# Two more 2 MB stretches of a rotation kernel's stores written with 8 KB rows in place of 16 KB

## The chip, the cores and the metric

The kernel runs on one core of one Trainium2 chip. The metric is the device time of one execution in microseconds (us), and the time of a kernel is the median of its runs. One execution was also recorded by the hardware profiler; its page and trace are what this text reads.

## The reference

```python
def setup_inputs():
    batch, c, h, w = 32, 3, 256, 256
    return {"x": np.random.randn(batch, c, h, w).astype(np.float32)}

def reference(x):
    return np.rot90(x, k=-1, axes=(-2, -1)).astype(np.float32)
```

Each of the 96 images of 256 x 256 float32 is turned by a quarter: 25.17 MB are read, the same number of bytes is written, and nothing is calculated.

## The kernel before

**Tiling.** The rows of all images are one list, `(b c h) w`. With R = 16 rows of an image to a partition, a *slab* is 128 partitions x 4096 elements (E), 16 KB on each partition and 2 MB in all. The 12 slabs stand in five groups of 2, 2, 2, 4 and 2 slabs (`sizes`), and each group has an SBUF tile of its own (`groups[n]`, `u` in the profile) that is loaded, turned in place and stored. So all 25 MB fit, and no buffer is used twice.

**Loads** are all issued by SyncE (SP) at the start. Group 0 comes in three DMAs with 8 KB rows (L55, L56: two of 1 MB, one of 2 MB). The others come with one DMA of 2 MB for each part of the partitions (L66), with rows of 16 KB, or 32 KB in the four-slab group; the very last is split in two of 1 MB (L63, L64). A row here is one contiguous run of bytes, and the trace shows one DMA packet for each.

**Turning.** VectorE transposes 32 x 32 blocks (L72, L88, L93). The first quarter of a slab pair goes to a spare tile, as its place is still needed, and ScalarE copies it back at the end (L78, L98). A group can be stored when VectorE and ScalarE are through with it. The four-slab group has eight such copies, the others fewer.

**Stores** are issued by SP in the order of the groups, each group in two halves: `a` is the parity of the partition (`groups[n][a::2]`, 64 partitions). For a two-slab group a half is 2 MB, for the four-slab group 4 MB, and its rows are 16 KB, the whole of a slab on one partition (L117). Only the first half of group 0 is split, in two stores of 1 MB that each write 8 KB rows, first the lower half of every slab's columns and then the upper (L109). The first store of all also waits for the last load but one (`mark`), so that stores do not push in among loads.

**What orders the DMAs.** All 25 DMAs go out on SP's one queue, in program order. The framework gives them eight semaphores in turn, so from the ninth on each DMA waits for the one eight places before it. SP ends (L143) with a row of wait instructions on these semaphores, and then a gather and release among the engines ends the program.

Of the kernel before, what the change touches and what calls it, by code (L numbers as in the profile page):

```python
# [1 line left out]

# [4 lines left out]


@with_exitstack  # L10
def kernel(
    ctx: ExitStack,
    tc: tile.TileContext,
    x: bass.AP,
    out: bass.AP,
):

    nc = tc.nc
    fp32 = mybir.dt.float32

    B, C, H, W = x.shape
    P = nc.NUM_PARTITIONS
    R = 16  # L30
    E = R * W
    hw = R // 2
    low, high = slice(0, hw), slice(hw, R)

    rows_in = x.rearrange("b c h w -> (b c h) w")
    rows_out = out.rearrange("b c h w -> (b c h) w")

    sizes = (2, 2, 2, 4, 2)
    first = [sum(sizes[:n]) for n in range(len(sizes))]
    groups = [  # L40
        ctx.enter_context(tc.tile_pool(name=f"group{n}", bufs=1)).tile([P, s, E], fp32, name=f"u{n}")
        for n, s in enumerate(sizes)
    ]
    psum = ctx.enter_context(tc.tile_pool(name="psum", bufs=1, space=bass.MemoryType.PSUM))
    spare = [psum.tile([P, E // 2], fp32, name=f"spare{h}") for h in range(2)]
    extra = ctx.enter_context(tc.tile_pool(name="extra", bufs=1)).tile([P, E // 2], fp32, name="extra")

    def rows_of(rows, n):
        return rows[first[n] * P * R : (first[n] + sizes[n]) * P * R]


    ld = rows_of(rows_in, 0).rearrange("(s i p r) w -> s i p (r w)", s=2, i=2, p=P)
    home = [groups[0][:, s].rearrange("p (i f) -> p i f", i=2) for s in range(2)]
    for i in range(2):
        nc.sync.dma_start(out=home[0][:, i], in_=ld[1, i])  # L55
    nc.sync.dma_start(out=home[1], in_=ld[0].transpose([1, 0, 2]))  # L56
    for n in range(1, len(sizes)):
        I = sizes[n]
        ld = rows_of(rows_in, n).rearrange("(a i m r) w -> i m a (r w)", a=2, i=I, m=P // I)
        to = groups[n].rearrange("p s f -> p (s f)").rearrange("p (a f) -> p a f", a=2)  # L60
        for i in range(I):
            if (n, i) == (len(sizes) - 1, I - 1):
                mark = nc.sync.dma_start(out=to[i::I, 0], in_=ld[i][:, 0])  # L63
                nc.sync.dma_start(out=to[i::I, 1], in_=ld[i][:, 1])  # L64
            else:
                nc.sync.dma_start(out=to[i::I], in_=ld[i])  # L66

    def turn_slab(src, dsts):
        s = src.rearrange("p (i r g c) -> p c r g i", i=2, r=R // 2, c=R)
        for h, d in enumerate(dsts):  # L70
            d = d.rearrange("p (c k r) -> p c r k", c=hw, r=R // 2)[:, :, ::-1, ::-1]
            nc.vector.transpose(out=d, in_=s[:, h * hw : (h + 1) * hw])  # L72

    u = groups[0]
    turn_slab(u[:, 0], spare)
    turn_slab(u[:, 1], [u[:, 0, : E // 2], u[:, 0, E // 2 :]])
    for h in range(2):
        nc.scalar.copy(out=u[:, 1, h * E // 2 : (h + 1) * E // 2], in_=spare[h])  # L78

    def turn_group(n, held):  # L80
        I = sizes[n]
        T = I // 2
        K = W // (R * T)
        u = groups[n].rearrange("p s f -> p (s f)")
        src = u.rearrange("p (a t r g c) -> p t c r g a", a=2, t=T, r=R, c=R)
        dst = u.rearrange("p (i c k t r) -> p t c r k i", i=I, c=R, k=K, t=T)[:, ::-1, :, ::-1, ::-1, :]
        for t in range(T):
            nc.vector.transpose(  # L88
                out=held[t].rearrange("p (i c k r) -> p c r k i", i=I, c=hw, k=K)[:, :, ::-1, ::-1, :],
                in_=src[:, t, low, low])  # L90
        for c, r in ((low, high), (high, high), (high, low)):
            for t in range(T):
                nc.vector.transpose(out=dst[:, t, c, r], in_=src[:, t, c, r])  # L93
        back = u.rearrange("p (i c k t r) -> p t i c k r", i=I, c=R, k=K, t=T)[:, ::-1]
        for t in range(T):
            kept = held[t].rearrange("p (i c k r) -> p i c k r", i=I, c=hw, k=K)
            for i in range(I):
                nc.scalar.copy(out=back[:, t, i, low, :, high], in_=kept[:, i])  # L98

    for n, held in enumerate(([extra], [spare[1]], spare, [extra]), 1):  # L100
        turn_group(n, held)


    st = rows_of(rows_out, 0).rearrange("(s i m r) w -> i m s (r w)", s=2, i=2, m=P // 2)
    for a in range(2):

        for f in ((low, high) if a == 0 else (slice(0, R),)):
            f = slice(f.start * W, f.stop * W)
            put = nc.sync.dma_start(out=st[a][:, :, f], in_=groups[0][a::2, :, f])  # L109
            if f.start or a:  # L110
                continue
            tc.add_manual_dep(put.ins, mark.ins.name, mybir.DependencyInfo(
                mybir.DependencyClass.Sync, mybir.DependencyReason.SCHED_ONLY), reason="stores after loads")
    for n in range(1, len(sizes)):
        st = rows_of(rows_out, n).rearrange("(a i m r) w -> a m i (r w)", a=2, i=sizes[n], m=P // 2)
        for a in range(2):
            nc.sync.dma_start(out=st[a], in_=groups[n][a::2])  # L117


# [1 line left out]
_INS = ['x']  # L121
_OUTS = [((32, 3, 256, 256), 'float32')]


# [23 lines left out]
```

## Time and profile before

| | |
|---|---|
| median of 3 runs | 123.1 us (123.0 to 123.1) |
| the profiled execution | 123.22 us |
| its span | 121.4 us |
| VectorE busy | 87.4 us, 24 instructions |
| ScalarE busy | 14.9 us, 17 instructions |
| DMA packets | 3600, of them 400 under 512 B |
| bytes moved | 50.33 MB, mean 414 GB/s over the span |
| time of the packets | 97.7% of 16 DMA engines' span |
| first store issued | 59.47 us |
| last store issued | 98.71 us |

The busy table gives each engine's time and share of the span. The slices cut the span in 40 and give each engine's busy share in tenths; the DMA row is the mean over the core's 16 DMA engines. The waits say who waited for whom, with the total, the number and the longest; "SPq" is SP's sequencer, which issues the DMAs. The view of DMA issues gives size and the time from issue to landing, which includes the time in which a DMA stands behind others in the queue.

### The profile page before, as it was taken

To read this page: it belongs to the slowest core of one execution; us is meant where nothing else is said; L and a number is where in the kernel's file an instruction comes from. 1 tells how busy PE (TensorE), PEld (TensorE's weight loads), DVE (VectorE), ACT (ScalarE), POOL (GpSimd) and SP (SyncE) were. 2 spreads that over 40 slices of the span, in tenths; PEclk is the share of its full clock that TensorE was granted. 3 is DMA by queue.
4 is the path that set the end of the run, shared out by engine and by line. 5 is a ranking of instruction groups with operands and counts; after the bars stand their busy time and mean duration, and the time that the engine had idled before them with its cause. 6 is when DMAs were issued, how large, how long until landed. Compare 5 with 4: busy or idle time off the path is not lost.

```text
span 121.4 us, 132 instructions
## 1 busy us (share of the span) xinstructions
DVE 87.4 (72%) x24; ACT 14.9 (12%) x17; POOL 0.2 (0%) x4
## 2 busy tenths in 40 slices
DVE  0039999999999999999999999999999600000000
ACT  0000400380005100060000000327000320000000
POOL 0000000000000000000000000000000000000000
DMA  3999999999989898999989999999999999999994
GB/s 70 432 429 426 456 432 432 432 432 432 518 345 518 345 518 345 432 432 432 426 378 453 432 432 432 432 432 432 405 416 426 432 432 432 432 432 432 432 426 178
DMA packets 3600, 50.33 MB, mean 414 GB/s; under 512 B 400, under 2 KB 400, under 8 KB 400
## 3 DMA queue, kind: packets, MB, share of 16 engines
q1 hardware_dynamic: 3600, 50.33, 97.7%
HBM read 25.17 MB, written 25.17 MB: 414 GB/s over the span
## 4 chain that ended last, share of the span: by engine, by line
DVE 66%; issue 6%; DMA 6%; ACT 1%; ACTq 1%; SPq 0%; DVEq 0%
DVE u L93 39%; DVE spare L88 9%; DVE extra L88 6%; DVE u L72 6%; DVE spare L72 6%; DMA u<-in_x_dram 6%; ACT u L98 1%; ACTq L143 1%; SPq L55 0%; DVEq L88 0%; DVEq L72 0%
## 5 line engine op out<-in xcount | busy, mean ns | idle before, releaser
L93 DVE STREAM_TRANSPOSE u<-u 128x2048 f32<-128x2048 f32 x15 | 54.4, 3651 | 0.4
L72 DVE STREAM_TRANSPOSE spare<-u 128x2048 f32<-128x2048 f32 x2 | 7.1, 3585 | 8.2 <-DMA u<-in_x_dram 8.2
L98 ACT COPY u<-spare 128x512 f32<-128x512 f32 (+1 forms) x10 | 6.0, 688 | 38.5 <-DVE u L93 38.5
L88 DVE STREAM_TRANSPOSE spare<-u 128x2048 f32<-128x2048 f32 x3 | 10.7, 3585 | 0.0
L88 DVE STREAM_TRANSPOSE extra<-u 128x2048 f32<-128x2048 f32 x2 | 8.0, 4011 | 0.0
L72 DVE STREAM_TRANSPOSE u<-u 128x2048 f32<-128x2048 f32 x2 | 7.8, 3986 | 0.0
L98 ACT COPY u<-extra 128x1024 f32<-128x1024 f32 x4 | 4.0, 1043 | 22.8 <-DVE u L93 22.8
L78 ACT COPY u<-spare 128x2048 f32<-128x2048 f32 x2 | 3.6, 1871 | 8.7 <-DVE u L72 8.7
L78 ACT ACT_TABLE_LOAD x1 | 1.3, 1283 | 13.1 <-DMA u<-in_x_dram 13.1
L132 POOL MEMSET const-bfloat16-1.0<- 128x1 bf16 x1 | 0.1, 101 | 0.0
L132 POOL MEMSET const-uint8-127<- 128x1 uint8 x1 | 0.1, 101 | 0.0
L132 POOL MEMSET const-float32-0.0<- 128x1 f32 x1 | 0.1, 98 | 0.2 <-issue 0.2
L132 POOL MEMSET const-float32-1.0<- 128x1 f32 x1 | 0.1, 98 | 0.0
## 6 DMA issues: line engine op xcount, KB each, us to landing
u<-in_x_dram SPq DMA_DIRECT2D x10, 2048.0 KB, 30.4
out_dram<-u SPq DMA_DIRECT2D x7, 2048.0 KB, 17.6
out_dram<-u SPq DMA_DIRECT2D x2, 4096.0 KB, 21.2
u<-in_x_dram SPq DMA_DIRECT2D x4, 1024.0 KB, 20.5
out_dram<-u SPq DMA_DIRECT2D x2, 1024.0 KB, 5.7
```

What stands on the lines that cost most here:

```text
L72: nc.vector.transpose(out=d, in_=s[:, h * hw : (h + 1) * hw])
L78: nc.scalar.copy(out=u[:, 1, h * E // 2 : (h + 1) * E // 2], in_=spare[h])
L88: nc.vector.transpose(out=held[t].rearrange("p (i c k r) -> p c r k i", i=I, c=hw, k=K)[:, :, ::-1, ::-1, :], in_=src[:, t, low, low])
L93: nc.vector.transpose(out=dst[:, t, c, r], in_=src[:, t, c, r])
L98: nc.scalar.copy(out=back[:, t, i, low, :, high], in_=kept[:, i])
L132: nc = _bacc.Bacc("TRN2", target_bir_lowering=False, num_devices=1)
L143: with _tile.TileContext(nc) as tc:
```

## The change

The stores of groups 1 to 4 are issued by this loop. For the four-slab group (n = 3) and the last group (n = 4), the first two slabs of the first half are now stored as two DMAs of 1 MB, each with half of every slab's columns, so with 8 KB rows. What is left of the half, two slabs of the four-slab group and nothing of the last group, goes out as one store with 16 KB rows. The second halves, and groups 0, 1 and 2, are as before. There are 28 DMAs in place of 25.

```diff
     for n in range(1, len(sizes)):
-        st = rows_of(rows_out, n).rearrange("(a i m r) w -> a m i (r w)", a=2, i=sizes[n], m=P // 2)
+        I = sizes[n]
+        st = rows_of(rows_out, n).rearrange("(a i m r) w -> a m i (r w)", a=2, i=I, m=P // 2)
         for a in range(2):
-            nc.sync.dma_start(out=st[a], in_=groups[n][a::2])
+            done = 0
+            if a == 0 and n >= 3:
+
+                done = 2
+                for f in (slice(0, E // 2), slice(E // 2, E)):
+                    nc.sync.dma_start(out=st[a][:, :done, f], in_=groups[n][a::2, :done, f])
+            if done < I:
+                nc.sync.dma_start(out=st[a][:, done:], in_=groups[n][a::2, done:])
```

## The prediction

> **What bounds the kernel now.** I read the page's busy table and its slices first: they say which engine is short of time. VectorE is busy 72% and is done by slice 32; the DMA row has a 9 or an 8 in every slice but the first and last.
>
> ```profile
> DVE 87.4 (72%) x24; ACT 14.9 (12%) x17; POOL 0.2 (0%) x4
> ...
> DVE  0039999999999999999999999999999600000000
> ...
> DMA  3999999999989898999989999999999999999994
> ...
> q1 hardware_dynamic: 3600, 50.33, 97.7%
> ```
>
> The packets of the one queue take 97.7% of 16 DMA engines' span. So the kernel is bound by moving 50.33 MB, and the page's chain (which follows VectorE and stops at 98 us) is not the chain that sets the end. What waits at the end is in the waits of SP's queue:
>
> ```profile
> SPq L109 <- DMA u<-in_x_dram: 31.2, 1, 31.2
> SPq L117 <- DVE u L93: 22.8, 2, 13.3
> SPq L143 <- DMA out_dram<-u: 20.3, 2, 19.6
> ```
>
> SP's last act (L143) is to wait 19.6 us at a stretch for stores that are long issued. Its timeline says when the last four stores, the ones that the change touches, were issued:
>
> ```profile
> 84.37 15.74 SPq L117 DMA_DIRECT2D out_dram<-u  x4
> ```
>
> And the view of DMA issues, asked for one issue at a time, says how long each took to land. The four rows are the store issued at 66.64 (the last one ahead of the four-slab group), the four-slab group's first half (issued 84.37), its second half (85.02) and the kernel's last store (98.71):
>
> ```profile
> out_dram<-u SPq DMA_DIRECT2D x1, 2048.0 KB, 24.5
> ...
> out_dram<-u SPq DMA_DIRECT2D x1, 4096.0 KB, 16.6
> ...
> out_dram<-u SPq DMA_DIRECT2D x1, 4096.0 KB, 25.8
> ...
> out_dram<-u SPq DMA_DIRECT2D x2, 2048.0 KB, 19.8
> ```
>
> (In the last row x2 is a wait for the median of the last two: 17.6 and 21.9.) Issue plus time to landing: the store ahead lands at 66.64 + 24.5 = 91.1, so at 84.37, when the four-slab group becomes ready, the queue still holds 6.8 us of work; that group lands at 101.0 and 110.8, so at 98.06, when the last group is ready, it holds 12.7 us. The last store lands at 98.71 + 21.9 = 120.6, and the span ends at 121.4. From first load to last landing the engines are never without work: joining the trace's packet records (start, duration, size) end to end gives engines whose packets overlap by 4 to 8 ns, with no gap over 60 ns once all are running. Two things can therefore change the time: what a packet costs, and the 0.8 us behind the last landing.
>
> **The change, part by part.**
>
> *What it does to the queue.* Of the four-slab group's first 4 MB store, the first two slabs (2 MB) go as two 1 MB stores of 8 KB rows and the other 2 MB as one store of 16 KB rows; of the last group, the first 2 MB store goes as two of 1 MB, 8 KB rows. Bytes are the same. Packets follow rows: 128 rows of 16 KB become 256 of 8 KB, twice, so +256, and each of the three added DMAs adds 16 completion packets (the page has 400 under 512 B for 25 DMAs), +48: 3904 for 3600. Nothing moves on VectorE or ScalarE. In the built program, the first store of each of the two groups waits for the same VectorE and ScalarE counts as before.
>
> *Price of a row.* From the packet records, mean duration by stage: 8 KB loads (3 to 12.9 us) 309.2 ns; 8 KB stores (61.6 to 66 us) 309.4; 16 KB stores right behind those (66.8 to 84) 611.5; 16 KB at 87 to 98 us, 615.4; at 101 to 120 us, 615.7. Per engine the change turns 2 x 8 rows of 16 KB into 32 of 8 KB: 16 x (2 x 309.4 - 615.5) = 16 x 3.3 = +0.05 us. Completion packets are 9 ns each, three more per engine, at most +0.03. Landings say less: the pair of 8 KB stores of 1 MB, its extra completion packet included, landed 4.90 us after the load ahead of it (median engine), and late 2 MB stores of 16 KB land 4.90 apart, so 0. I take **+0.02**, between the two, nearer to the landings, since they hold all of it. Ends: 0 and +0.16: the dearest row of 8 KB that the trace has is the 2 MB load of L56, 4.97 us against 4.89 for the 16 KB loads, 0.08 for each of the two.
>
> *What 16 KB rows cost behind 8 KB rows.* The one thing that speaks for the change. Rows of 16 KB took 611 both times that they ran right behind 8 KB rows (loads from 13 us: 611 to 613; stores from 66.8: 611.5), and about 615.5 everywhere else. The stores stayed at 611 until about 84.4, just when SP issued the next stores, and the loads crept up from 13 to 18 us, when SP issued loads; between 87 and 120 nothing brought 611 back. I read this as: 8 KB rows put the engines in step, a burst of issues puts them out. That is a reading, not a shown cause. By it the new kernel gains 4 ns a row from the end of the 8 KB part in the four-slab group (91.1 + 4.9 = 96.0) to the next issues at 98.06, 2 us or 3.4 rows, -0.01; and for the last 2 MB, 8 rows, behind which nothing is issued, -0.03. Sum **-0.04**. Ends: 0, if it isn't so; and if issues don't undo it, 6 MB + 2 MB = 32 rows by up to 7 ns (the packets' distances fall from 614 at most to 607), -0.22.
>
> *Issues.* Three more of them on SP, 0.65 us each (L109's 8 KB stores took 672 and 650 ns); behind them waits only SP, and the queue holds 6.8 and 12.7 us of work meanwhile. Nothing, as long as that cover holds. Rows during a burst of two issues (98.0 to 100.7) took 619.7, 4 ns over the rest for 4 rows: three more issues could add 0.03; I count 0 and keep 0.03 for the upper end. From the ninth on each DMA also waits for the one eight before it; for the stores of these two groups those landed at 62 to 86 us, so before the groups are ready.
>
> The Trainium skill ("SBUF — State Buffer", section "The DMA setup-cost knee") speaks against the change: every transfer pays a roughly fixed 2 us, so one big transfer beats several. By that, three more transfers would cost an estimated 6 us, and the time would be 129. This trace differs where the queue is full: the two 1 MB loads of the last group landed 2.47 and 2.45 us after the DMA before each, half of the 4.89 of a 2 MB load. The measurement decides, and the sum has nothing for it.
>
> *Behind the last landing.* At the end SP runs five wait instructions on the eight DMA semaphores, one after the other, in a fixed order that begins with the fourth semaphore. DMAs take the eight in turn. Before, the 25th and last DMA is on the first semaphore, which stands in the fourth of the five waits; one more wait follows. With 28 DMAs the last is on the fourth semaphore, in the **first** of the five, and four waits follow the last landing: three more. Each is short but serial. In SP's instruction records the wait behind the last landing starts 35 ns after the one before ended and takes 28, 63 together; two of these waits that had nothing to wait for started 59 ns apart. 3 x 60 = **+0.18 us**, straight onto the end: SP's drain, GpSimd's gather and the release all stand behind it. Ends: 0 (if SP looks through satisfied waits while another is pending, for which no row speaks) and +0.19.
>
> *Sum.* +0.02 - 0.04 + 0.18 = **+0.16 us**. The profiled execution took 123.22 us (span 121.4 and 1.8 around it), so 123.38 by its own time; it ran 0.1 above the median of 123.1, so 123.26 by that, and I say **123.25**. That is +0.12%: less than the 0.2% (0.25 us) that a measurement of this kernel can tell from no change.
>
> **Rivals.**
> 1. *The 8 KB rows do what they seem to have done at 66 us, and it lasts.* For it: 611.5 for 17 us of stores. Against it: it ended at the next burst of issues. 32 rows at -4 to -7 ns, -0.14 to -0.22, rows +0.02, tail +0.18: -0.02 to +0.06, time 123.1.
> 2. *Same, and the tail is free.* Then -0.12 to -0.20: 122.95. Faster by over 0.2% (below 122.85) it is only with the rows at nothing and the gain at its end.
> 3. *Slower: 8 KB rows cost here what they cost in loads.* Place: the two 2 MB parts at 91 to 96 and 110.8 to 115.7 us. Price: 0.08 us each, as L56's load, +0.16 in place of +0.02; nothing regained, issues +0.03, tail +0.18: +0.37, 123.45. It decides once the two parts together cost over 0.07 us (tail 0.18, and nothing gained). Against it: the 8 KB stores at 62 to 66 us landed at the pace of 16 KB ones.
> 4. *It doesn't do what it says:* the smaller stores might have been able to leave earlier than the big one, as they need fewer copies. The built program waits for the same counts, and the queue is 6.8 us deep anyway. Time then by tail alone: 123.3 at most.
>
> **How the numbers follow.** Forecast (123.15 to 123.35, with rival 4) 0.55; rivals 1 and 2 as far as they stay between 122.85 and 123.15, 0.20; rival 2 below that, 0.03; rival 3 and all else from 123.35 up, 0.22. Faster by over 0.2%: 0.03. Slower by over 0.2%: 0.22. Within: 0.75. The range leaves out rival 2's lower part and what lies beyond rival 3: 122.95 to 123.45.
>
> **What would show it.** Right: 3904 packets, 448 of them under 512 B; SP's last wait for stores ends, and four short waits instead of one follow; landing to end of span 1.0 us for 0.8. 16 KB rows of the last 2 MB at 611. Wrong: DMA engines with gaps, so a cover that failed; 8 KB rows over 312 ns; 16 KB rows that stay at 611 past 98 us; a last landing before 120.4 or after 120.8.

## The result, and the profile after

The changed kernel takes **123.44 us** (123.36 to 123.68, 6 runs), the kernel before, beside it, 123.07 (122.95 to 123.12): a ratio of 1.0035, interval 1.0023 to 1.0048. It is slower by 0.37 us, or 0.3%: over twice the +0.16 of the forecast, which had given 0.75 to a time within 0.2% of the kernel before. The profiled execution took 123.68 us, the longest of the six, span 121.9.

The busy table and the packet counts of the page of after:

```profile
DVE 87.4 (72%) x24; ACT 14.9 (12%) x17; POOL 0.2 (0%) x4
...
DMA  3999999999989999999999999999999999999993
...
DMA packets 3905, 50.33 MB, mean 413 GB/s; under 512 B 449, under 2 KB 449, under 8 KB 449
...
q1 hardware_dynamic: 3904, 50.33, 97.6%
q14 instruction: 1, 0.00, 0.0%
```

The compute engines are as they were, and the queue is as full: 3904 packets, 448 small ones (the 3905th is an instruction fetch). So the added issues left no hole in the queue. Where the time came from is in two other views. First the DMA issues of after, one at a time: the two 8 KB stores of the four-slab group (issued at 84.33 and 84.98) and the 16 KB store behind them (86.42):

```profile
out_dram<-u SPq DMA_DIRECT2D x1, 1024.0 KB, 9.4
...
out_dram<-u SPq DMA_DIRECT2D x1, 1024.0 KB, 11.2
...
out_dram<-u SPq DMA_DIRECT2D x1, 2048.0 KB, 14.7
```

They land at 93.7, 96.2 and 101.1: 2.5 us for each 1 MB in 8 KB rows, 4.9 for the 2 MB in 16 KB rows, and the first pair of 8 KB stores, at 62 to 66 us, had taken 4.90 together. In the landing records (median engine) the two new pairs took 5.00 and 4.99, and what stands behind them 4.89 (2 MB), 9.80 (4 MB) and 4.87. In the kernel before 2 MB took 4.89 (half of the first 4 MB) and 4.90, and the second 4 MB 9.78. So the 8 KB rows cost 0.1 us a pair and gave nothing back. From the landing of the last load to that of the last store (the stores' part below) the median engine took 58.59 us before and 58.76 after, **+0.17**. (From the first load's landing to the last one's it is 56.25 to 56.26 in both.)

Second, SP's wait instructions at the program's end, first of before, then of after (number, shortest/median/longest in ns, first and last start):

```profile
L143 SPq EVENT_SEMAPHORE  x7: 17/28/9787, 100.2 to 121.4; - x7
```

```profile
L151 SPq EVENT_SEMAPHORE  x7: 17/28/28, 120.8 to 121.8; - x7
```

Before, SP went through its waits from 100.2 us on and sat 9.8 us in the fourth. After, the first wait is the long one. The view of SP's waits has it, with the total, the number and the longest:

```profile
SPq L151 <- DMA out_dram<-u: 19.4, 1, 19.4
```

So all five are passed behind the last landing at 120.82. Their starts are 58, 67, 65 and 61 ns apart. From the last landing to the end of the span it is 0.85 us before and 1.07 after, **+0.21**. Together +0.38, against the 0.37 of the medians. The two profiled spans are 0.45 apart: in that one execution the loads also landed 0.06 earlier, and the last engine came 0.13 further behind the median one. So such parts, each from one execution, are good to 0.1 or 0.2 us.

### The profile page after: what moved, and what is told of

It reads as the page before. It is cut to its first block, busy times and chain, and to the rows that moved or that the text cites. A ratio compares the mean times of both kernels' runs of the same rounds, so it can differ in the third digit from the quotient of the medians.

```text
span 121.9 us, 135 instructions
## 1 busy us (share of the span) xinstructions
DVE 87.4 (72%) x24; ACT 14.9 (12%) x17; POOL 0.2 (0%) x4
## 3 DMA queue, kind: packets, MB, share of 16 engines
q1 hardware_dynamic: 3904, 50.33, 97.6%
## 4 chain that ended last, share of the span: by engine, by line
DVE 66%; issue 6%; DMA 6%; ACT 1%; ACTq 1%; SPq 0%; DVEq 0%
DVE u L93 39%; DVE spare L88 9%; DVE extra L88 6%; DVE u L72 6%; DVE spare L72 6%; DMA u<-in_x_dram 6%; ACT u L98 1%; ACTq L151 1%; SPq L55 0%; DVEq L88 0%; DVEq L72 0%
```

## The experiments

The theory, formed on the result (A): the change costs two things of about equal size, a fixed time per packet for 16 more data packets on each engine, and three waits behind the last landing. The rivals: the number of DMAs costs (B), the row size costs all and the waits nothing (C), 8 KB rows bring later rows back to 611 ns (D, the prediction's reading), the 8 KB rows were dear for their place (E).

**28 DMAs, rows of 16 KB** (e1). The changed kernel, its 1 MB stores cut by slab:

```diff
-                for f in (slice(0, E // 2), slice(E // 2, E)):
-                    nc.sync.dma_start(out=st[a][:, :done, f], in_=groups[n][a::2, :done, f])
+                for s in range(done):
+                    nc.sync.dma_start(out=st[a][:, s : s + 1], in_=groups[n][a::2, s : s + 1])
```

> The changed kernel with its four small stores cut by slab in place of by column: 28 DMAs of the same sizes as in the changed kernel, but all the late rows are 16 KB. Theory A (two halves: extra packets at about 12 ns each per engine, and three more waits behind the last landing at 63 ns each): the rows' half goes, the waits' half stays, +0.19 to +0.22 us on the kernel before (123.27). Rival B (more DMAs, with their issues and completions, are what costs; row size is nothing): +0.37, as the changed kernel. Rival C (it is all row size; the waits behind the last landing cost nothing): 0.0 to +0.03.

123.28 us, ratio 1.0021 (1.0012 to 1.0029): +0.22. The same DMAs with 16 KB rows keep 0.22 of 0.37. Rows alone are the other 0.16. Against B and C.

**32 DMAs, rows of 16 KB** (e2): as e1, with `if n < 3 or a == 0:` for `if a == 0 and n >= 3:`, and both halves of groups 1 and 2 are stored as two 1 MB DMAs.

> As the run with 28 DMAs of 16 KB rows, and the first two groups behind group 0 are also stored slab by slab: 32 DMAs, so that the last one is on the eighth semaphore, which stands in the last of the five waits. Theory A: no wait follows the last landing, 0.06 less than before; seven more DMAs add seven completion packets of 9 ns per engine, up to +0.06: -0.06 to 0.0 us (123.05). Rival B (DMAs cost): +0.37 x 7/3 = +0.9. Rival C: 0.0 to +0.06.

122.93 us, ratio 0.9993 (0.9984 to 1.0002): -0.13. Four DMAs *more* than e1 and 0.35 us *less*. SP's waits of e1, then of e2:

```profile
L151 SPq EVENT_SEMAPHORE  x7: 17/28/28, 120.3 to 121.3; - x7
```

```profile
L151 SPq EVENT_SEMAPHORE  x7: 17/28/28, 101.4 to 121.1; - x7
```

In e2 four of the five waits were passed by the time of the last landing, and the end of the span is 0.81 us behind it, in e1 1.07. That is 0.25 of the 0.35; the other 0.10 is in the stores' part, which A had not foreseen (it said -0.06 to 0.0). B is out.

**No 8 KB stores** (e3): `for f in (slice(0, R),):` at L107, 24 DMAs.

> The kernel before with the first half of group 0 stored as one DMA of 16 KB rows: no store has 8 KB rows, 24 DMAs. Theory A (a packet costs a fixed 7 to 12 ns and 8 KB rows do nothing else): 8 packets less per engine, -0.06 to -0.10, one wait less behind the last landing, -0.06: -0.12 to -0.17 us (122.92). Rival D (8 KB rows bring the engines in step, which was worth 4 ns on each of the 32 rows behind them): that gain goes, +0.13, and +0.0 in sum (123.07), with 16 KB stores at 615 from the start.

123.0 us, ratio 0.9994 (0.9985 to 1.0003): -0.06, between the two and so not decided by the time. The end is 0.04 shorter (A: 0.06), but the stores' part is not shorter (+0.02): the first 2 MB landed in 4.88 us for 4.90, so the early 8 KB pair had cost 0.02, and not A's 0.06 to 0.10. In the packet records, with no 8 KB store ahead, the 16 KB stores between 62 and 84 us took a median of 611 ns and a mean of 613.4. D had said 615. The mean lies between 611 and 615, but the same code with its 8 KB stores gave 611.5 in the kernel before and 613.9 in the changed one (67 to 84 us), so this is no sign of D; e6 settles it.

**All stores in 8 KB rows** (e4):

```diff
-        for f in ((low, high) if a == 0 else (slice(0, R),)):
+        for f in (low, high):
...
-            nc.sync.dma_start(out=st[a], in_=groups[n][a::2])
+            for f in (slice(0, E // 2), slice(E // 2, E)):
+                nc.sync.dma_start(out=st[a][:, :, f], in_=groups[n][a::2, :, f])
```

> Every store in 8 KB rows, by halves of the columns: 34 DMAs, 88 packets more per engine than before. Theory A: 88 x 7 to 12 ns = +0.62 to +1.06, the last DMA on the second semaphore, so one wait more behind the last landing, +0.06, nine completion packets +0.08 at most: +0.7 to +1.2 us (124.0). Rival D (in step after 8 KB rows, so that all stay at 309): the lower end, 0.6. Rival E (the changed kernel's 8 KB rows were dear for their place, at 91 and 111 us, not for their number): rows at 309 but in those places, 16 + 16 packets at 12 and 56 at 3 ns, +0.4 with the wait.

124.09 us, ratio 1.0087 (1.0073 to 1.0101): +1.03. Its page:

```profile
DMA packets 5152, 50.33 MB, mean 412 GB/s; under 512 B 544, under 2 KB 544, under 8 KB 544
```

The stores' part rose by 1.01 us for 88 more data packets per engine, 11.5 ns each. That is a mean: by the landings the second 2 MB, with 8 more packets, cost nothing (4.85 us for 4.87), the next two groups 16 ns for each added packet, the four-slab group 12 and the last 9. The 8 KB rows took a mean of 310 ns up to 66 us, 312.5 to 84, 318 to 90 and 314 from 103 on, though only 8 KB rows had run: the dearer packets of the later part aren't mended by 8 KB rows, and the price is not confined to the two places that the change touched (E).

**No late bursts of issues** (e5): the kernel before with `if n < 3:` over `turn_group(n, held)`, so the last two groups are left unturned.

> The kernel before without the turning of the last two groups, which are stored as they were loaded; so no store waits for work after 70 us, all of them are issued by about 73 us, and no burst of issues falls at 84 or 98 us. DMAs, rows and bytes are as before. Theory A with the reading of the prediction (a burst of issues is what takes a packet from 611 to 615): rows stay at 611 up to the end, 66 rows of 4.5 ns and the two bursts' own 0.1 us: -0.3 to -0.4 us (122.7). Rival F (the dearer packets come with the place, the data's addresses or the time since the start, not with the bursts): rows go to 615 from about 84 to 95 us all the same, only the bursts' own time goes, -0.05 to -0.1 us (123.0).

123.02 us, ratio 0.9995 (0.9986 to 1.0003): -0.02, far from A's -0.3 to -0.4 and less than F's -0.05 to -0.1. The rows were at 611 until 71 us, rose to 614.3 (mean) at 84 to 90 us and 615.6 from 103 on, without any issue after about 74 us. So the other half of the prediction's reading, that the issues at 84 us made the rows dear, falls too, and F's rows are what came; only the peak at 98 to 103 us (619.5 in the kernel before, 615.7 here) goes with the issues.

**What the runs pointed to** (e6): stores with 16 KB rows only, two-slab groups stored slab by slab, the four-slab group in two halves, 32 DMAs.

```diff
-            nc.sync.dma_start(out=st[a], in_=groups[n][a::2])
+            k = sizes[n] if n == 3 else 1
+            for s in range(0, sizes[n], k):
+                nc.sync.dma_start(out=st[a][:, s : s + k], in_=groups[n][a::2, s : s + k])
```

and likewise group 0, by slab.

> What the runs so far point to: no store in 8 KB rows, every two-slab group stored slab by slab in 1 MB DMAs, the four-slab group in two halves: 32 DMAs, the last on the semaphore that is waited for last. Theory A: against the run with 32 DMAs (122.93), 8 packets fewer per engine at 7 ns: 122.88, so -0.18 us on the kernel before. Rival D (the 8 KB rows of group 0 keep the later rows at 611): 32 rows or more by 4 ns, +0.1 on that run, 123.05.

**122.87 us, ratio 0.9981 (0.9973 to 0.9990): faster than both kernels**, by 0.17 and 0.57 us. It ends like e2 (0.82 us behind the last landing), its 16 KB rows stay at 611 until 98 us (mean 611.0 at 90 to 98, where before had 614.8), right through the issues at 84 us, and the stores' part is 58.37 us, 0.22 less than before. D is out: no 8 KB store, and the longest stretch at 611.

**The change with 32 DMAs** (e7): the changed kernel, groups 1 and 2 by slab as in e2, so that no semaphore wait of a DMA follows the last landing.

> The changed kernel, its 8 KB rows as they are, with the two groups behind group 0 stored slab by slab: 32 DMAs, so that no wait for another semaphore follows the last landing. Theory A (63 ns for each of the four waits): 0.25 less than the changed kernel, 123.19, and by the steadier rows of the other run with 32 DMAs up to 0.1 less, 123.1. Against that run (122.93) the only difference is 8 KB for 16 KB rows in 4 MB, 16 packets per engine: +0.12 to +0.19. Rival C (waits cost nothing): as the changed kernel, 123.44. Rival B (DMAs cost): 0.5 more, 123.9.

123.19 us, ratio 1.0014 (1.0005 to 1.0024): 0.25 less than the changed kernel, as A said. SP's waits:

```profile
L155 SPq EVENT_SEMAPHORE  x7: 17/28/28, 102.1 to 121.9; - x7
```

The last landing, at 121.15, ends the fifth and last of the waits, and the span ends 0.81 us later. Against e2, which differs by the 8 KB rows alone, it is +0.26, more than the 0.12 to 0.19 expected. In the landings 0.16 of it is in the two 8 KB pairs; the rest is spread over 16 KB stores ahead of them and behind, which both kernels issue alike.

**4 KB rows in the same 4 MB** (e8):

```diff
-                for f in (slice(0, E // 2), slice(E // 2, E)):
+                for q in range(4):
+                    f = slice(q * E // 4, (q + 1) * E // 4)
```

> The changed kernel with 4 KB rows in the same 4 MB: four DMAs of 512 KB in place of two of 1 MB, 32 in all, so nothing follows the last landing. Theory A (a packet costs a fixed 12 ns): 48 packets per engine over the kernel before, +0.58, waits -0.06, seven completions up to +0.06: +0.5 to +0.6 us (123.6). Rival G (it is the cut into two column halves, not the number of packets): as much as with 8 KB rows without the waits, +0.13 to +0.19 (123.2).

123.49 us, ratio 1.0035 (1.0023 to 1.0047): +0.45, a little under the expected 0.5 to 0.6, and far over G's 0.2. Its page has the 1024 packets of 4 KB and the 512 completion packets:

```profile
DMA packets 4480, 50.33 MB, mean 413 GB/s; under 512 B 512, under 2 KB 512, under 8 KB 1536
```

In the trace the stores' part is 0.58 us longer, 12 ns for each of 48 added data packets per engine. So the price goes with the number of packets, not with the cut by columns (G).

**Why 611 here and 615 there** (e9 to e12). e6 left open whether it was the slab-by-slab order or the size of the DMAs. e9 stored the four-slab group by slab too and needed four DMAs of 32 partitions to come to 40; e10 was e6 with its 1 MB stores cut by partition:

```diff
-            k = sizes[n] if n == 3 else 1
-            for s in range(0, sizes[n], k):
-                nc.sync.dma_start(out=st[a][:, s : s + k], in_=groups[n][a::2, s : s + k])
+            k = 64 if n == 3 else 32
+            for m in range(0, 64, k):
+                nc.sync.dma_start(out=st[a][m : m + k], in_=groups[n][a + 2 * m : a + 2 * (m + k) - 1 : 2])
```

> As the fastest run so far (32 DMAs, 122.87), with the four-slab group also stored slab by slab and the last group's first half in four DMAs of 512 KB: 40 DMAs, rows of 16 KB, the last DMA again on the semaphore waited for last. If storing one slab at a time is what keeps rows at 611: the 30 rows or so per engine from 99 us on lose 3 to 4 ns each, -0.1, and eight more completion packets of 9 ns add up to +0.07: 122.77 to 122.84, rows at 611 up to 120 us. If rows become dearer anyway late in the run: 122.87 to 122.94.

> As the fastest run so far (32 DMAs, 122.87), with its 1 MB stores cut by partition in place of by slab: each has both slabs of 32 partitions, so its rows alternate between two places in the output 1 MB apart (2 MB in group 0). Same number of DMAs and packets, same waits. If storing one slab at a time is what keeps rows at 611: rows go to 615 by 84 to 95 us as in the kernel before, 20 to 40 rows by 4 ns, +0.1: 122.97. If it is the size or number of the DMAs: 122.87.

128.18 us (ratio 1.0375, 1.0344 to 1.0407) and 145.29 us (1.1822, 1.1775 to 1.187): neither theory, both far off. The cut by partition had brought in something new. e11 and e12 are the same kernels with each of those DMAs on every fourth partition of all 128 (`st[a][m::k]` from `groups[n][a + 2 * m :: 2 * k]`) in place of every second partition of one half.

> The run with 40 DMAs by slab again, its four 512 KB DMAs cut so that each takes every fourth partition over all 128, in place of every second of one half. If it was the half of the partitions that made those packets up to twice as long: 122.77 to 122.84 when storing one slab at a time keeps the rows at 611, 122.87 to 122.94 when they become dearer late in any case. If a DMA of 32 partitions is slow by itself: 128 again.

> The run with 1 MB stores of two slabs and 32 partitions again, each now of every fourth partition over all 128. If the half of the partitions was the cause, its 22 us go. Then, against 122.87 of the run with the same DMAs by slab: 122.97 and rows at 615 by 84 to 95 us if storing one slab at a time is what keeps them at 611; 122.87 if it is the size or number of the DMAs.

123.04 us (1.0001, 0.9993 to 1.0010) and 123.0 us (0.9991, 0.9982 to 1.0000): the 5 and 22 us are gone. Windows of e10, then of e12 (the last two columns are the DMA engines' busy share and GB/s):

```profile
64.00:74.00 10.00, 9.93 (x4) 0.00 (x0) 0.00 (x0) 1.00 0.96 224
```

```profile
64.00:74.00 10.00, 9.93 (x4) 0.00 (x0) 0.00 (x0) 1.00 1.03 437
```

With each DMA on one half of the partitions it is half the rate, with DMA engines that look busy all the same: the packets themselves took about twice as long at first (a mean of 1303 ns at 62 to 66 us, in e12 611). The Trainium skill has this ("SBUF — State Buffer", section "Door 1: The DMA port swizzle"): partitions 0 to 63 reach only half of the SBUF ports, and the page's bound for that is 218 GB/s. The 224 here lies 3% above it.

For the question itself: at 84 to 90 and 90 to 98 us, e12, with two slabs to a DMA, had rows of 620.7 and 615.0 ns, and e11, with one, 612.3 and 612.2, both with stores of 16 KB rows only. With e2 (612.9 at 84 to 90 us) and e6 (611.2) this speaks for storing one slab at a time, as e12's expectation had it. It isn't shown, for three reasons. e7 issues the same stores as e2 up to 91 us and had 616.1. From 91 us on e6 stores four slabs in turn, and its rows were still at 611.0. And the times don't follow: run side by side, e11 took 123.04 and e12 123.0, where e11 was expected at 122.77 to 122.94. The traced executions are no help: e11's is as long as e6's (span 121.2 us in both), which was the longest of e6's runs. What its eight more DMAs or the four of 512 KB cost in the median is open. From 103 us on even e6 and e11 had 614. What makes a row dearer by 4 ns late in the run is not settled.

## Why the prediction was wrong, by its steps

The sum of the parts and the runs. "Stores" is the stores' part against before, "end" what lies behind the last landing against before, both in the profiled execution, and "time" the medians' difference, in us:

| run | stores | end | sum | time |
|---|---|---|---|---|
| changed kernel | +0.17 | +0.21 | +0.38 | +0.37 |
| e1: 28 DMAs, 16 KB | +0.04 | +0.21 | +0.25 | +0.22 |
| e2: 32 DMAs, 16 KB | -0.06 | -0.04 | -0.10 | -0.13 |
| e3: no 8 KB stores | +0.02 | -0.04 | -0.02 | -0.06 |
| e4: all 8 KB | +1.01 | +0.06 | +1.07 | +1.03 |
| e5: quiet end | -0.04 | 0.00 | -0.04 | -0.02 |
| e6: all 16 KB, 32 DMAs | -0.22 | -0.04 | -0.26 | -0.17 |
| e7: the change, 32 DMAs | +0.21 | -0.04 | +0.17 | +0.15 |
| e8: 4 KB, 32 DMAs | +0.58 | -0.04 | +0.54 | +0.45 |
| e11: 40 DMAs, by slab | -0.16 | -0.04 | -0.20 | -0.01 |
| e12: 32 DMAs, two slabs | +0.10 | -0.04 | +0.06 | -0.05 |

- *What bounds the kernel*: right. In these runs the packets took 97.4 to 98.1% of the DMA engines' span, and the stores' part plus the end gives the time within 0.11 us, but for e11 (0.19).
- *Price of a row*: this step failed. It said +0.02, and the two pairs measured +0.19 in the landings against e1's (5.00 and 4.99 us, with 16 KB rows 4.90 and 4.90) and +0.16 in the time. The working compared unlike rows: 8 KB rows from an undisturbed stretch (309.4 ns) with 16 KB rows from a disturbed one (615.5), a difference of 3.3 ns a pair. Like with like it is 2 x 309.4 - 611.5 = 7.3 in the early stretch and 2 x 313.8 - 615.5 = 12.1 in the late one, where the change puts its rows; 16 x 12.1 ns = 0.19 us. The late surcharge of some 4 ns sits on each *packet*, of 8 KB as of 16, so halving the rows doubles it. That could be worked out from the trace of before: its loads between 30 and 58 us, in a disturbed stretch too, took 614.5 ns for 16 KB and 1216.2 for 32, so 2 x 614.5 - 1216.2 = 12.8 for one packet more. The lean towards the landings of the first pair (+0) made it worse, as these too were early (e3: 0.02 for that pair). Of its own signs of being wrong two came: 8 KB rows over 312 ns (313.6 and 314.0 in the new pairs) and a last landing after 120.8 (120.82).
- *What 16 KB rows cost behind 8 KB rows*: -0.04 forecast, nothing measured. Behind the new 8 KB rows the landings took 4.89, 9.80 and 4.87 us (e1, without them, 4.93, 9.78 and 4.88), and the 16 KB rows of the last 2 MB 615.5 ns, not 611. The reading was wrong in both halves: 611 comes without 8 KB stores (e6), and the rows grow dear without issues (e5). Rivals 1 and 2 rested on it too.
- *Issues*: right, none seen: in e1, with as many issues, the 1 MB stores of 16 KB rows landed 4.90 us a pair, as one of 2 MB did. The first of the new stores was issued at 84.33 us, against 84.37, so rival 4's earlier start didn't come.
- *Behind the last landing*: right in mechanism, +0.18 said, +0.21 measured; e1, e2 and e7 show it by moving the last DMA from one semaphore to another.
- *Rival 3* had the size (+0.37) and nearly the parts: 0.16 for the rows, priced from the load of L56, where +0.19 was measured, and 0.18 for the waits, where it was +0.21. That its total is exact is luck: the 0.03 that it put on the issues was not there.

## What to carry to other kernels

When a DMA queue is full from end to end, count packets per engine and price each at the fixed part of its duration (from two row sizes *in the same stretch* of the trace); here 7 to 13 ns, so 8 KB in place of 16 KB costs 1 to 2% of what it touches. Then look behind the last landing: which semaphore the last DMA is on, and how many waits stand behind it, moved this kernel by up to 0.25 us, and adding or removing DMAs shifts it by chance. Before reading a cause into a change of pace along one trace, see whether a run without the supposed cause shows it too, and how far two executions of the same code differ (here by 2 to 3 ns a row).

## What the runs showed of the hardware that was not expected

- The time that a packet costs beyond its bytes matters at 8 KB: 11.5 to 12 ns on average by the landings of e4 and e8. The Trainium skill ("DMA: Bandwidth & Descriptors", section "Why small descriptors are slow (HBM only)") names a fixed overhead of some 3 cycles a packet; at the 850 MHz that the page gives for the fabric that is an estimated 3.5 ns. These two averages are over three times as much.
- DMAs on 32 partitions within one half of SBUF moved 224 GB/s (e10, 64 to 74 us), the same on 32 spread partitions 437 (e12).
- Waits that are already satisfied aren't free at the end of a program: 58 to 67 ns each on SP, in series (the changed kernel).
- 16 KB rows can stay at 611 ns up to 98 us (e6), where the kernel before had 615. It came with stores of one slab at a time ahead, but e7 (616.1 for e2's 612.9 with the same stores) leaves it unshown, and why is open.
